# The MLP up projection with the activations stationary instead of the weights, its result turned by 32x32 block transposes and transfers inside SBUF

## The chip, the cores and the metric

The kernel runs on one core of one Trainium2 chip. The metric is the device time of one execution in microseconds (us), as the median of several runs. The rows below come from one profiled execution.

## The reference, cut to what matters

A two-layer decoder trunk on 256 tokens of width 2048, in float32. Each layer is a normalised attention mixer with a residual, and after it a normalised squared-ReLU MLP with a residual:

```python
D_MODEL = 2048; SEQ = 256; DEPTH = 2; D_FF = 4 * D_MODEL
def sq_relu_mlp(h, w_up, w_down):
    return jnp.square(jax.nn.relu(h @ w_up)) @ w_down
...
for layer in range(DEPTH):
    hn = rms_norm(h, ln_mix_g[layer])
    h = h + (even_mixer or odd_mixer)(hn, ...)
    hn = rms_norm(h, ln_mlp_g[layer])
    h = h + sq_relu_mlp(hn, w_mlp_up[layer], w_mlp_down[layer])
```

The change touches the MLP of both layers: up is 256 x 2048 by 2048 x 8192, down is 256 x 8192 by 8192 x 2048.

## The kernel before, in words

**Products.** Each float32 operand is split into a high part in fp32r and the rest, and three products stand for one: high x high, high x low, low x high. The normalised activations lie transposed in `xT` (128 channels of a k-tile in the partitions, the 256 tokens of both parts beside each other); `big` holds the MLP's hidden activations in the same form, `hid(b)` being the half of it that belongs to block `b`.

**Weights.** Everything that TensorE multiplies is a list of units. A weight chunk of 1 MB (four k-tiles of 512 columns) comes by one DMA on SyncE's queue into one of three `raw` buffers (`load`, L233). Each unit is half a chunk (two k-tiles): ScalarE writes its high part `wh` (L243), VectorE the rest `wl` (L244), into one of four buffers each. `run()` writes the program out by hand: before unit `u` it emits the split of unit `u + 3`, and the load of the chunk that replaces a wholly split one; then it emits the unit's matmuls. A unit yields four times, and at each yield (a slot) `bg.slot` emits up to two steps of side tasks that are due. The order on each engine is the order of emission, and so is the order of SyncE's queue.

**The MLP.** The 8192 hidden channels of a layer are 8 blocks of 1024, each of two halves `g` of 512. The order is up(0), up(1), down(0), up(2), down(1) and so on, down(7). A half of an up block goes through `b_units` (L347 to L390): the weights are stationary, and for each of 16 k-tiles and each of four groups of 128 channels the high weights meet both parts of x (512 columns, L370) and the low weights meet the high part (256 columns, L367). The result has the channels in the partitions, as down needs it. Four evacuations each add the two parts, take the squared ReLU and split it into `hid(b)` (L801 to L808). Banks 0 to 3 serve g = 0, banks 4 to 7 serve g = 1.

Down (L813) and the attention's projections go through `a_units` (L279): x is stationary, 128 tokens of it at a time, and 512 columns of weights move: six matmuls for one k-tile, one for each of three products and two token halves `hf`. The unit in the middle of a run emits them by L319, the first and the last unit by L306 to L308. The result has the tokens in the partitions. Down's four column groups `n` use banks 2n and 2n + 1.

Of the kernel before, what the change touches and what calls it, by code (L numbers as in the profile page):

```python
# [12 lines left out]
AF = mybir.ActivationFunctionType  # L13
ALU = mybir.AluOpType
AX = mybir.AxisListType

S = 256
# [3 lines left out]
KT = D // 128  # L21
# [126 lines left out]
def trunk_kernel(ctx: ExitStack, tc: tile.TileContext, x, w_up, w_down, even_w_in, even_w_out,  # L148
                 odd_w_in, odd_w_out, k_w1, k_w2, v_w1, v_w2, vec, rows, con, rot_in, ident_in, out):
    nc = tc.nc  # L150
# [4 lines left out]
    def sb(name, shape, dt=F32):  # L155
        return pool.tile(shape, dt, name=name)

    bank = [psum.tile([128, 512], F32, name=f"bank{i}") for i in range(8)]
# [7 lines left out]
    NRAW, NHL = 3, 4  # L166
    raw = [sb(f"raw{i}", [128, 2048]) for i in range(NRAW)]
    wh = [sb(f"wh{i}", [128, 1024], F32R) for i in range(NHL)]
    wl = [sb(f"wl{i}", [128, 1024], F32R) for i in range(NHL)]
    T = [sb(f"t{i}", [128, 1024]) for i in range(10)]  # L170
# [31 lines left out]
    bg = Background()  # L202


    units = []
# [6 lines left out]
    def weight_chunk(w, k0, nk, segs):  # L212

        width = sum(n for _, n in segs)
        pieces, at = [], 0
        for c0, n in segs:
            src = w[k0 * 128:(k0 + nk) * 128, c0:c0 + n].rearrange("(k p) c -> p k c", p=128)
            pieces.append((nk, width, at, n, src))
            at += n
        return chunk(pieces)  # L220
# [104 lines left out]
    def wide_units(w, segs, lhs, evac, banks, pre):  # L325


        for i0 in range(0, KT, 2):
            ci = weight_chunk(w, i0, 2, segs)
            for k in (i0, i0 + 1):  # L330
# [12 lines left out]
                            yield  # L343

                units.append((ci, (k - i0) * 1024, 1024, gen, True))

    def b_units(w, c0, rhs, evac, banks, pre=None):  # L347


        state = {}  # L350
        for i0 in range(0, KT, 4):
            ci = weight_chunk(w, i0, 4, [(c0, 512)])
            for j0 in (0, 2):
                ks = [i0 + j0, i0 + j0 + 1]

                def gen(u, ks=ks):
                    first, last = ks[0] == 0, ks[-1] == KT - 1
                    if pre:
                        pre(ks)
                    if first:  # L360
                        state["banks"] = banks()
                    h = wh[u % NHL].rearrange("p (k c) -> p k c", c=512)
                    lo = wl[u % NHL].rearrange("p (k c) -> p k c", c=512)
                    def part(j, n, lo_part):
                        o, k = state["banks"][j], ks[n]
                        if lo_part:
                            nc.tensor.matmul(o[:, :S], lo[:, n, j * 128:(j + 1) * 128], rhs(k)[:, :S], start=False,  # L367
                                             stop=last and n == 1)
                        else:
                            nc.tensor.matmul(o, h[:, n, j * 128:(j + 1) * 128], rhs(k), start=first and n == 0, stop=False)  # L370

                    if first or last:
                        for j in range(4):
                            for n in range(2):
                                part(j, n, 0)
                                part(j, n, 1)
                            if last:
                                evac(j, state["banks"][j])
                            yield
                    else:  # L380
                        steps = [(j, n) for n in range(2) for j in range(4)]
                        for i, (j, n) in enumerate(steps):
                            part(j, n, 0)
                            if i:
                                part(*steps[i - 1], 1)
                            if i == 7:
                                part(j, n, 1)
                            if i % 2:
                                yield

                units.append((ci, j0 * 512, 1024, gen, True))

    def t_units(w, c0, m, rhs, evac, pre):

# [92 lines left out]
    def rotate(name, of):  # L487
        rot[name] += 1
        return of[(rot[name] - 1) % len(of)]
# [4 lines left out]
    class Prep:  # L494
# [7 lines left out]
        def evac(self, hf, ps):  # L502
            r = self.norm.rows()
            if hf == 0 and self.src.name in owner:
                bg.need(owner[self.src.name])
            q = self.src[:, hf * 512:(hf + 1) * 512]
            sq = SQ[hf]
            nc.scalar.activation(q, ps, AF.Copy, scale=r[:, hf:hf + 1])
            nc.scalar.activation(sq, ps, AF.Square, scale=r[:, 2 + hf:3 + hf])
            nc.vector.tensor_reduce(self.ms[:, hf * 4:hf * 4 + 4], sq.rearrange("p (h d) -> p h d", h=4), AX.X, ALU.add)  # L510
            if hf == 1:
                self.task = owner[self.src.name] = bg.spawn(self.rest(), 2)
# [144 lines left out]
    heads = {}  # L657
# [103 lines left out]
                in_proj([(3 * FOX_W + blk * 512, 512)], gate_evac, n0)  # L761


    def out_proj(w, ready, norm, passes):
        def bl(k, part, hf):
            return big[:, k, part, hf * 128:(hf + 1) * 128]

        for first, last in passes:
            for n in range(NB):
                def evac(hf, ps, n=n, last=last):  # L770
                    xd = xs[:, hf, n * 512:(n + 1) * 512]
                    nc.vector.tensor_tensor(xd, ps, xd, ALU.add)
                    if last < KT:
                        return
                    norm.square(n, hf)
                    if hf == 1:
                        norm.start(n, (bank[4 + 2 * (n % 2)], bank[5 + 2 * (n % 2)]), 4)
                        if n == NB - 1:
                            norm.rtask = bg.spawn(stats(norm), 4)

                a_units(w, [(n * 512, 512)], bl, list(range(first, last)), evac, main3, ready)
# [5 lines left out]
    def mlp(layer, norm, nxt):  # L787
        up, down = w_up[layer], w_down[layer]
        NBLK = DFF // 1024

        def hid(b):
            return big[:, (b % 2) * 8:(b % 2) * 8 + 8]

        def up_units(b):
            for g in range(2):
                def evac(j, ps, g=g):
                    k = g * 4 + j
                    t, s_, q_ = T[j][:, 0:S], T[j][:, S:2 * S], T[j][:, 2 * S:3 * S]
                    if ("hid", j) in heads:
                        bg.need(heads["hid", j])  # L800
                    nc.scalar.activation(t, ps[:, S:], AF.Copy)  # L801
                    nc.vector.tensor_tensor(s_, ps[:, :S], t, ALU.add)
                    nc.vector.scalar_tensor_tensor(q_, s_, 0.0, s_, op0=ALU.max, op1=ALU.mult)  # L803

                    def rest():
                        d = hid(b)
                        nc.scalar.activation(d[:, k, 0], q_, AF.Copy)  # L807
                        nc.vector.tensor_tensor(d[:, k, 1], q_, d[:, k, 0], ALU.subtract)  # L808
                        yield 2
                    heads["hid", j] = bg.spawn(rest(), 1 + j)  # L810
                b_units(up, b * 1024 + g * 512, xr, evac, lambda g=g: bank[4:8] if g else [bank[3]] + [rotate("main", bank[0:3]) for _ in range(3)], norm.need)

        def down_units(b):  # L813
            for n in range(NB):
                bks = (bank[2 * n], bank[2 * n + 1])

                def evac(hf, ps, n=n):
                    if n == 0 and hf == 0 and b == 0:
                        bg.need(norm.rtask)
                    xd = xs[:, hf, n * 512:(n + 1) * 512]  # L820
                    nc.vector.scalar_tensor_tensor(xd, ps, norm.r2[:, hf:hf + 1], xd, op0=ALU.mult, op1=ALU.add)  # L821
                    if b < NBLK - 1:
                        return
                    if nxt is not None:
                        nxt.square(n, hf)
                        if hf == 1:
                            m = 2 * ((n + 3) % 4)
                            nxt.start(n, (bank[m], bank[m + 1]), 4)
                            if n == NB - 1:
                                nxt.rtask = bg.spawn(stats(nxt), 4)  # L830
                    else:
                        nc.sync.dma_start(out[hf * 128:(hf + 1) * 128, n * 512:(n + 1) * 512], xd)

                a_units(down, [(n * 512, 512)],
                        lambda k, part, hf: hid(b)[:, k - 8 * b, part, hf * 128:(hf + 1) * 128],
                        list(range(8 * b, 8 * b + 8)), evac, lambda bks=bks: bks,
                        lambda ks: bg.need(*[heads["hid", j] for j in range(4)]))

        for b in range(NBLK):
            up_units(b)  # L840
            if b:
                down_units(b - 1)
        down_units(NBLK - 1)
# [289 lines left out]
```

## Time and profile before

| what | value |
|---|---|
| median of 3 runs | 2297.97 us (2297.13 to 2299.61) |
| the profiled execution, its own time | 2299.28 us |
| its span in the profile | 2297.5 us |
| TensorE (matmul) busy | 2284.8 us, 99% |
| TensorE weight loads busy | 1924.0 us, 84% |
| VectorE busy | 1383.0 us, 60% |
| ScalarE busy | 1086.6 us, 47% |
| bytes moved, mean rate | 414.47 MB, 180 GB/s |
| mean granted TensorE clock | 0.999 |

Busy shares are means over the whole span. Matmuls are pipelined and overlap their weight loads, so the mean duration of one matmul is longer than the time by which it moves the next one on; the distance between starts, read from the chain that ended last, is the step.

### The profile page before, as it was taken

To read this page: it belongs to the slowest core of one execution; us is meant where nothing else is said; L and a number is where in the kernel's file an instruction comes from. 1 tells how busy PE (TensorE), PEld (TensorE's weight loads), DVE (VectorE), ACT (ScalarE), POOL (GpSimd) and SP (SyncE) were. 2 spreads that over 40 slices of the span, in tenths; PEclk is the share of its full clock that TensorE was granted. 3 is DMA by queue.
4 is the path that set the end of the run, shared out by engine and by line. 5 is a ranking of instruction groups with operands and counts; after the bars stand their busy time and mean duration, and the time that the engine had idled before them with its cause. 6 is when DMAs were issued, how large, how long until landed. Compare 5 with 4: busy or idle time off the path is not lost.

```text
span 2297.5 us, 28664 instructions
## 1 busy us (share of the span) xinstructions
PE 2284.8 (99%) x11403; PEld 1924.0 (84%) x11403; DVE 1383.0 (60%) x2075; ACT 1086.6 (47%) x1573; POOL 29.5 (1%) x28
## 2 busy tenths in 40 slices
PE   9999999999999999999999999999999999999999
PEld 7788888888888888888888888888888888888887
DVE  5565666666566566556554566756666556566564
ACT  6655554544444444444443555555444444444342
POOL 0000000000000000000000000000000000000000
PEclk9999999999999999999999999999999999999999
DMA  7455555555655555555546643335555565565654
GB/s 260 148 181 165 181 161 171 182 185 188 197 185 189 193 187 192 181 198 192 187 147 205 207 164 128 111 111 181 186 187 193 182 196 194 184 195 176 202 194 150
DMA packets 212870, 414.47 MB, mean 180 GB/s; under 512 B 10880, under 2 KB 12160, under 8 KB 212736
## 3 DMA queue, kind: packets, MB, share of 16 engines
q1 hardware_dynamic: 211728, 411.53, 55.0%
q8 instruction: 89, 1.46, 0.3%
q10 hardware_dynamic: 1008, 1.12, 0.1%
q14 instruction: 45, 0.37, 0.0%
HBM read 410.52 MB, written 2.10 MB: 180 GB/s over the span
## 4 chain that ended last, share of the span: by engine, by line
PE 97%; DVE 1%; ACT 1%; DMA 0%; issue 0%; ACTq 0%
PE bank L319 34%; PE bank L370 21%; PE bank L367 11%; PE bank L306 8%; PE bank L308 8%; PE bank L307 8%; PE bank L646 1%; PE bank L618 1%; PE bank L641 1%; PE bank L910 1%; PE bank L339 1%; PE bank L340 1%; PE bank L537 1%; DVE wl L244 1%; PE bank L455 1%; PE bank L338 1%
## 5 line engine op out<-in xcount | busy, mean ns | idle before, releaser
L244 DVE TENSOR_TENSOR wl<-raw,wh 128x1024 fp32r<-128x1024 f32 (+1 forms) x771 | 938.3, 1221 | 770.2 <-ACT wh L243 767.9
L243 ACT ACTIVATE wh<-raw 128x1024 fp32r<-128x1024 f32 (+1 forms) x771 | 812.3, 1055 | 864.9 <-PE bank L370 320.9
L370 PE MATMUL bank<-xT,wh 128*128 128x512 f32 x2048 | 707.6, 398 | 0.0
L367 PE MATMUL bank<-xT,wl 128*128 128x256 f32 x2048 | 543.5, 281 | 0.0
L370 PEld LDWEIGHTS bank<-xT,wh 128*128 128x128 f32 x2048 | 372.0, 188 | 74.9
L367 PEld LDWEIGHTS bank<-xT,wl 128*128 128x128 f32 x2048 | 386.9, 189 | 18.4
L319 PE MATMUL bank<-wh,big 128*128 128x512 f32 x1280 | 358.9, 391 | 0.0
L319 PE MATMUL bank<-wh,xT 128*128 128x512 f32 x1056 | 296.7, 394 | 0.0
L319 PEld LDWEIGHTS bank<-wh,big 128*128 128x128 f32 x1280 | 239.7, 188 | 49.1 <-DVE big L655 0.2
L306 PE MATMUL bank<-wh,big 128*128 128x512 f32 x640 | 253.1, 395 | 0.0
L308 PE MATMUL bank<-wh,big 128*128 128x512 f32 x640 | 249.7, 390 | 0.0
L307 PE MATMUL bank<-wl,big 128*128 128x512 f32 x640 | 249.6, 390 | 0.0
L319 PEld LDWEIGHTS bank<-wh,xT 128*128 128x128 f32 x1056 | 196.7, 188 | 39.2
L319 PE MATMUL bank<-wl,big 128*128 128x512 f32 x640 | 202.9, 393 | 0.0
L319 PE MATMUL bank<-wl,xT 128*128 128x512 f32 x528 | 172.7, 397 | 0.0
L308 PEld LDWEIGHTS bank<-wh,big 128*128 128x128 f32 x640 | 120.3, 188 | 25.6 <-DVE big L655 0.4
L306 PEld LDWEIGHTS bank<-wh,big 128*128 128x128 f32 x640 | 120.4, 188 | 24.3 <-ACT big L654 0.2
L319 PEld LDWEIGHTS bank<-wl,big 128*128 128x128 f32 x640 | 120.2, 188 | 24.4
L307 PEld LDWEIGHTS bank<-wl,big 128*128 128x128 f32 x640 | 120.5, 188 | 23.5
L319 PEld LDWEIGHTS bank<-wl,xT 128*128 128x128 f32 x528 | 99.2, 188 | 20.2 <-issue 0.2
L821 DVE SCALAR_TENSOR_TENSOR xs<-bank,r_m,xs 128x512 f32<-128x512 f32 x128 | 89.9, 743 | 7.8 <-PE bank L308 7.8
L807 ACT ACTIVATE big<-t 128x256 fp32r<-128x256 f32 x128 | 52.6, 415 | 81.8 <-DVE t L803 81.8
(189 smaller groups left out, 1543.3 us busy)
## 6 DMA issues: line engine op xcount, KB each, us to landing
raw<-in_w_up SPq DMA_DIRECT2D x128, 1024.0 KB, 5.3
raw<-in_w_down SPq DMA_DIRECT2D x128, 1024.0 KB, 5.1
raw<-in_even_w_in SPq DMA_DIRECT2D x48, 1024.0 KB, 5.1
raw<-in_odd_w_in SPq DMA_DIRECT2D x40, 1024.0 KB, 5.1
raw<-in_even_w_out SPq DMA_DIRECT2D x16, 1024.0 KB, 5.0
raw<-in_odd_w_out SPq DMA_DIRECT2D x16, 1024.0 KB, 5.3
raw<-in_even_w_in SPq DMA_DIRECT2D x10, 512.0 KB, 5.5
raw<-in_even_w_in SPq DMA_DIRECT2D x12, 256.0 KB, 5.1
```

The source lines that it names most:

```text
L243: nc.scalar.activation(h[:, at], r[:, at], AF.Copy)
L244: nc.vector.tensor_tensor(lo[:, at], r[:, at], h[:, at], ALU.subtract)
L306: nc.tensor.matmul(o, lhs(k, 0, hf), h[:, n], start=st, stop=False)
L307: nc.tensor.matmul(o, lhs(k, 0, hf), lo[:, n], start=False, stop=False)
L308: nc.tensor.matmul(o, lhs(k, 1, hf), h[:, n], start=False, stop=last and n == len(ks) - 1)
L319: nc.tensor.matmul(bks[hf], lhs(k, part, hf), w_[:, n], start=False, stop=False)
L338: nc.tensor.matmul(o, lhs(k, 0, hf), h[:, at], start=k == 0, stop=False)
L339: nc.tensor.matmul(o, lhs(k, 0, hf), lo[:, at], start=False, stop=False)
L367: nc.tensor.matmul(o[:, :S], lo[:, n, j * 128:(j + 1) * 128], rhs(k)[:, :S], start=False, stop=last and n == 1)
L370: nc.tensor.matmul(o, h[:, n, j * 128:(j + 1) * 128], rhs(k), start=first and n == 0, stop=False)
L807: nc.scalar.activation(d[:, k, 0], q_, AF.Copy)
L821: nc.vector.scalar_tensor_tensor(xd, ps, norm.r2[:, hf:hf + 1], xd, op0=ALU.mult, op1=ALU.add)
```

## The change

`b_units` goes. The up projection goes through `a_units` with `xl` as stationary operand: per half block and k-tile six matmuls of 512 columns, with banks 4 and 5 for g = 0, and 6 and 7 for g = 1. Its result has tokens in the partitions, and has to be turned:

- After each token half `hf`, VectorE's `blocks` transposes the bank's 4 x 4 grid of 32x32 blocks per 128 channels into half of `T[g]` (one instruction for 128x512 elements, read from PSUM in permuted order).
- When both halves are there, a side task emits sixteen transfers on SyncE's queue in four steps two slots apart (`across`): each moves 32 partitions of `T[g]`, two runs of 128 elements per partition, to another 32 partitions of `T[2 + g]`, 32 KB in all.
- Twenty-two slots after the last of the four steps (29 after the evacuation), VectorE takes the squared ReLU of the whole 128x1024 tile in place. Two slots later ScalarE writes the high part of it into `hid(b)`, and VectorE the rest.

Down of block `b` then waits for the two tasks of its own block, under keys of their own, and the evacuation of half `g` waits for the task of the block before on that half.

```diff
-    def b_units(w, c0, rhs, evac, banks, pre=None):
...
+    def blocks(dst, src):
+        nc.vector.transpose(dst.rearrange("p (q j i) -> p q j i", q=4, j=4), src.rearrange("p (j q i) -> p q j i", j=4, q=4))
+
+    def across(dst, src, a):
+        for q in range(4):
+            nc.sync.dma_start(dst[32 * q:32 * q + 32].rearrange("i (s a c) -> i s a c", a=4, c=128)[:, :, a],
+                              src[32 * a:32 * a + 32].rearrange("i (s q c) -> i s q c", q=4, c=128)[:, :, q])
...
-                def evac(j, ps, g=g):
-                    k = g * 4 + j
-                    t, s_, q_ = T[j][:, 0:S], T[j][:, S:2 * S], T[j][:, 2 * S:3 * S]
-                    if ("hid", j) in heads:
-                        bg.need(heads["hid", j])
-                    nc.scalar.activation(t, ps[:, S:], AF.Copy)
-                    nc.vector.tensor_tensor(s_, ps[:, :S], t, ALU.add)
-                    nc.vector.scalar_tensor_tensor(q_, s_, 0.0, s_, op0=ALU.max, op1=ALU.mult)
+                def evac(hf, ps, g=g):
+                    turned_, d = T[g], T[2 + g]
+                    if b:
+                        bg.need(heads["hid", b - 1, g])
+                    blocks(turned_[:, hf * 512:(hf + 1) * 512], ps)
 
                     def rest():
-                        d = hid(b)
-                        nc.scalar.activation(d[:, k, 0], q_, AF.Copy)
-                        nc.vector.tensor_tensor(d[:, k, 1], q_, d[:, k, 0], ALU.subtract)
+                        for a in range(4):
+                            across(d, turned_, a)
+                            yield 2
+                        yield 20
+                        nc.vector.scalar_tensor_tensor(d, d, 0.0, d, op0=ALU.max, op1=ALU.mult)
                         yield 2
-                    heads["hid", j] = bg.spawn(rest(), 1 + j)
-                b_units(up, b * 1024 + g * 512, xr, evac, lambda g=g: bank[4:8] if g else [bank[3]] + [rotate("main", bank[0:3]) for _ in range(3)], norm.need)
+                        q = d.rearrange("p (s j t) -> p j s t", s=8, j=4)
+                        h, lo = (hid(b)[:, 4 * g:4 * g + 4, part].rearrange("p j (s t) -> p j s t", s=8) for part in range(2))
+                        nc.scalar.activation(h, q, AF.Copy)
+                        nc.vector.tensor_tensor(lo, q, h, ALU.subtract)
+                        yield 1
+                    if hf == 1:
+                        heads["hid", b, g] = bg.spawn(rest(), 1)
+
+                a_units(up, [(b * 1024 + g * 512, 512)], xl, list(range(KT)), evac,
+                        lambda g=g: (bank[4 + 2 * g], bank[5 + 2 * g]), norm.need)
...
-                        lambda ks: bg.need(*[heads["hid", j] for j in range(4)]))
+                        lambda ks: bg.need(*[heads["hid", b, g] for g in range(2)]))
```

## Rows read from the trace of the kernel before

**Rows 1.** The page's busy times per engine over the span, and the granted TensorE clock and the DMA share in 40 slices.
```profile
PE 2284.8 (99%) x11403; PEld 1924.0 (84%) x11403; DVE 1383.0 (60%) x2075; ACT 1086.6 (47%) x1573; POOL 29.5 (1%) x28
...
PEclk9999999999999999999999999999999999999999
DMA  7455555555655555555546643335555565565654
```

**Rows 2.** The page's chain that ended last, by engine and by line.
```profile
PE 97%; DVE 1%; ACT 1%; DMA 0%; issue 0%; ACTq 0%
PE bank L319 34%; PE bank L370 21%; PE bank L367 11%; PE bank L306 8%; PE bank L308 8%; PE bank L307 8%; PE bank L646 1%; PE bank L618 1%; PE bank L641 1%; PE bank L910 1%; PE bank L339 1%; PE bank L340 1%; PE bank L537 1%; DVE wl L244 1%; PE bank L455 1%; PE bank L338 1%
```

**Rows 3.** The chain in order of time (start, us, what): the middle pieces of down(0)'s four column groups and, after up(2), of down(1)'s first.
```profile
550.54 5.44 PE bank L319 x24
561.42 5.44 PE bank L319 x24
572.30 5.44 PE bank L319 x24
583.18 5.44 PE bank L319 x24
639.14 5.44 PE bank L319 x24
```

**Rows 4.** The same view in an attention projection of layer 0, where x is stationary from `xT` and the run has 16 k-tiles.
```profile
118.54 16.32 PE bank L319 x72
```

**Rows 5.** Busy time and count of each engine, granted clock, DMA share and rate over up(2) and over down(1).
```profile
591.20:636.40 45.20, 45.20 (x258) 39.37 (x257) 25.57 (x32) 19.63 (x25) 0.00 (x0) 1.00 0.59 193
636.40:680.00 43.60, 43.60 (x194) 36.09 (x193) 27.61 (x34) 19.14 (x24) 0.00 (x0) 1.00 0.59 189
```

**Rows 6.** Groups of instructions by line and shape over the span (count, busy us, mean ns of one, idle before): TensorE.
```profile
L370 PE MATMUL bank<-xT,wh 128*128 128x512 f32 x2048 | 707.6, 398 | 0.0
L367 PE MATMUL bank<-xT,wl 128*128 128x256 f32 x2048 | 543.5, 281 | 0.0
L319 PE MATMUL bank<-wh,xT 128*128 128x512 f32 x1056 | 296.7, 394 | 0.0
```

**Rows 7.** The same view: VectorE, the splits, what the change removes, and the nearest instructions to what it adds.
```profile
L244 DVE TENSOR_TENSOR wl<-raw,wh 128x1024 fp32r<-128x1024 f32 x767 | 935.7, 1224 | 768.6 <-ACT wh L243 766.3
L803 DVE SCALAR_TENSOR_TENSOR t<-t 128x256 f32<-128x256 f32 x128 | 54.4, 425 | 4.4
L802 DVE TENSOR_TENSOR t<-bank,t 128x256 f32<-128x256 f32 x128 | 53.4, 417 | 0.0
L808 DVE TENSOR_TENSOR big<-t,big 128x256 fp32r<-128x256 f32 x128 | 51.1, 420 | 15.5 <-ACT big L807 15.5
L772 DVE TENSOR_TENSOR xs<-bank,xs 128x512 f32<-128x512 f32 x32 | 20.9, 683 | 2.7 <-PE bank L308 2.7
L565 DVE RECIPROCAL t<-t 128x128 f32<-128x128 f32 x16 | 14.9, 939 | 0.1
L563 DVE TENSOR_SCALAR t<-t 128x512 f32<-128x512 f32 x4 | 1.6, 392 | 0.0
```

**Rows 8.** The same view: ScalarE.
```profile
L243 ACT ACTIVATE wh<-raw 128x1024 fp32r<-128x1024 f32 x767 | 810.0, 1057 | 862.7 <-PE bank L370 320.9 <-PE bank L319 315.3 <-PE bank L308 188.5
L807 ACT ACTIVATE big<-t 128x256 fp32r<-128x256 f32 x128 | 52.6, 415 | 81.8 <-DVE t L803 81.8
L801 ACT ACTIVATE t<-bank 128x256 f32<-128x256 f32 x128 | 43.9, 369 | 0.0
```

**Rows 9.** Instructions in order of time in down(1) (start, us, what, idle before and its releaser): a split on ScalarE, the same split on VectorE, and the next on ScalarE.
```profile
652.78 1.06 ACT L243 ACTIVATE wh<-raw 128x1024 fp32r<-128x1024 f32 x1 [1.66 <-PE bank L319]
655.50 1.06 ACT L243 ACTIVATE wh<-raw 128x1024 fp32r<-128x1024 f32 x1 [1.66 <-PE bank L319]
...
653.87 1.23 DVE L244 TENSOR_TENSOR wl<-raw,wh 128x1024 fp32r<-128x1024 f32 x1 [1.49 <-ACT wh L243]
```

**Rows 10.** Who waited for whom from 540 to 1130 us (engine, line, what it waited for: us in total, times, longest), all of the rows of that answer.
```profile
DVE wl L244 <- ACT wh L243: 228.7, 168, 1.6
ACT wh L243 <- PE bank L370: 132.2, 81, 1.8
ACT wh L243 <- PE bank L319: 85.8, 57, 1.7
ACT wh L243 <- PE bank L308: 82.6, 50, 1.7
ACT big L807 <- DVE t L803: 33.2, 26, 1.8
DVE big L808 <- ACT big L807: 6.3, 13, 0.5
```

**Rows 11.** Transfers: a weight DMA's issue on SyncE's queue (ns min/median/max) and its time to landing in the stretch 640 to 700 us; the page's medians for the twelve weight pieces of 256 KB at the start and for the eight output transfers of 256 KB; the queue's packets, MB and share of 16 engines.
```profile
L233 SPq DMA_DIRECT2D raw<-in_w_up x8: 367/368/368, 660.6 to 699.0; - x8
DMA to landing us min/median/max: 4.9/5.2/5.5
...
raw<-in_even_w_in SPq DMA_DIRECT2D x12, 256.0 KB, 5.1
out_x<-xs SPq DMA_DIRECT2D x8, 256.0 KB, 2.6
...
q1 hardware_dynamic: 211728, 411.53, 55.0%
```

**Rows 12.** SyncE's queue at the start (start, us, what), and one of its waits in the first 40 us.
```profile
4.84 0.39 SPq L189 DMA_DIRECT2D xs<-in_x  x1
5.36 2.65 SPq L233 DMA_DIRECT2D raw<-in_even_w_in  x4
...
SPq L189 <- DMA raw<-in_even_w_in: 1.0, 1, 1.0
```

More of the change, by code (lines that the diff above doesn't have):

```diff
@@ L345, in wide_units @@
                 units.append((ci, (k - i0) * 1024, 1024, gen, True))
-    def b_units(w, c0, rhs, evac, banks, pre=None):
[L350 to L391, printed above, removed]
     def t_units(w, c0, m, rhs, evac, pre):
```

## The prediction, made before the change was run

> **What bounds the kernel now.** I read the busy times first: TensorE is busy 99% of the span, every other engine 60% or less, and its clock is granted at 90% or more in every slice [rows 1], 1.00 of the 2.4 GHz level in the MLP stretches of [rows 5]. A busy TensorE may still be a waiting one, so I read the chain that ended last: 97% of it is TensorE, and the two lines of the up projection, L370 and L367, hold 21% and 11% [rows 2]. In the MLP there is no wait to remove: in 590 us of it TensorE waits for nobody, only ScalarE and VectorE wait, for TensorE and for each other, and nobody waits for a transfer [rows 10]. So the MLP's time is the number of TensorE's steps times the length of one, and the change can gain only by shortening that sum.
>
> The step's length is the third reading. The mean durations of a matmul (398, 281, 394 ns [rows 6]) are of no use for it, because neighbours overlap. The chain in order of time gives it. Down's column groups start 10.88 us apart (561.42 less 550.54) and hold 48 matmuls each: 226.7 ns a matmul. The middle pieces say the same, 5.44 us for 24 [rows 3]. From the middle of down(0)'s last group to the middle of down(1)'s first are 55.96 us (639.14 less 583.18); one column group of 10.88 us lies in it, and the rest, **45.08 us, is up(2)**: two half blocks of 22.54 us, each 128 matmuls. The 45.20 and 43.60 us windows over up and down, both with TensorE busy throughout, agree with 45.08 and 4 x 10.88 = 43.52 [rows 5].
>
> **What the change takes away.** A half block has 16 k-tiles. Before, a k-tile is 4 x (512 + 256) = 3072 columns in eight matmuls; after, 6 x 512 = 3072 columns in six. The columns stay; two instructions with their weight loads go. Before, a k-tile costs 22.54 / 16 = 1.409 us. After, the same six matmuls on the same `xT`, in the same helper, are what the attention projections run: 72 in 16.32 us, 226.7 ns each [rows 4], so a k-tile costs 1.360 us and a half block 96 x 0.2267 = 21.76 us. Its first and last units use another order (L306 to L308), which the 10.88 us groups of down already contain at the same mean [rows 3]. The gain is 0.78 us a half block; 8 blocks, 2 halves and 2 layers make 32: **25.0 us**.
>
> The page "TensorE: Matmul & The Clock Gate" of the Trainium skill, section "Back-to-back issue gap", counts 518 cycles for 512 columns and 262 for 256 at the full clock, as an isolated gap. By it, as an estimate, a k-tile goes from 3120 to 3108 cycles, 5 ns, and the whole change gains 2.6 us. The trace differs: 226.7 ns where that count gives 216, and 352 ns for a pair of 512 and 256 where it gives 325 (1.409 / 4, worked out above).
>
> **What it adds, and what hides it.** All of it lies on engines beside TensorE, so the question is how late each may be. A split ends on VectorE 2.3 us after the unit before which it was emitted begins (ScalarE's 1.06 and VectorE's 1.23 us from 652.78 to 655.10 [rows 9]); its unit comes three units later, and a unit is 2.72 us (655.50 less 652.78). TensorE stands only if a split is later than 8.16 - 2.3 = **5.8 us**. A weight chunk is sent for when a buffer's last split ends and is first read after two more chunks, 0.4 + 4 x 2.72 = 11.3 us later; it lands after 5.2 us at the median [rows 11], so it has **6.1 us** before ScalarE waits, and 5.8 more before TensorE does.
>
> - VectorE, removed per half block: 4 x (417 + 425 + 420) ns = 5.05 us [rows 7]. Added: two block transposes of 128x512 from PSUM, a squared ReLU and a subtraction of 128x1024. The trace has no transpose on VectorE. Bounds: 0.39 us (a 128x512 with one input in SBUF) and 3.76 us (the reciprocal's 939 ns per 128 elements, four times). I take 0.68, the row that also reads 128x512 from PSUM [rows 7]. The two others are of L244's shape, 1.22 us each. Sum 3.8 us, between 3.2 and 10.0: VectorE, busy 25.6 of 45.2 us in up now, would be at most 35 of 43.5 [rows 5]. The place matters more: the second transpose is ahead of the next split. At the dear end the two finish 6.2 us after the half block (the first may start 1.36 us, half a unit, before its end), the split's part follows at 7.4, and 8.16 is when it is due. So nothing at either end.
> - The later pair stands in VectorE's queue ahead of splits too: 1.22, then ScalarE's copy of 1.06, then 1.22: 3.5 us, under 5.8. Nothing.
> - ScalarE, removed: 4 x (369 + 415) = 3.1 us; added: one copy of 128x1024, near 1.06 [rows 8]. A relief off the path.
> - SyncE's queue gets sixteen transfers per half block, 512 in all. An issue takes 0.37 us [rows 11], so 5.9 us. They stand behind a weight load that waits for a split, about 3 us into the next half block, and ahead of the next load, which is ready at 7.7 us: by issues alone it is 1.2 us late. An issue may also wait for an earlier transfer that has nothing to do with it (SyncE stood 1.0 us before an x load for a weight transfer [rows 12]). If half of the sixteen had to wait for the weight load to land, the last would leave at 3 + 5.2 + 8 x 0.37 = 11.2 us and the next load be 3.9 us late. Both are under 6.1. Nothing; with that cover gone it would be TensorE that waits.
> - The turn itself: 28 slots of 0.68 us (a quarter of a unit) after the half block, at 19 us, VectorE reads the result. The last transfer leaves by 8.9 to 11.2 us. No row shows a 32 KB transfer inside SBUF; the nearest lands in 2.6 us, 256 KB from SBUF [rows 11], and behind a weight load 5.2 or more. Landed at 11.5 to 16.4: before 19. Nothing.
> - DMA engines: 1024 packets of 512 B per half block, 64 per engine. A 2 KB packet takes 0.55 x 16 x 2297.5 / 211728 = 95 ns of an engine [rows 11]; a quarter of it to all of it makes 1.5 to 6.1 us of 21.76, on a share of 0.59 [rows 5]: 0.66 to 0.87.
> - GpSimd's queue gets and loses nothing. Banks 4 to 7 in up were last read one column group of down earlier at the nearest. The down projection's wait on its own block costs nothing: half g = 1 is due 31 slots into the down of the block before, which has 64.
>
> The Trainium skill speaks against such transfers: "DMA: Bandwidth & Descriptors", section "Measured (HBM→SBUF, 128 partitions, SWDGE, issued from GpSimd)", has transfers under 64 KB dominated by their descriptors. At the 2 us of fixed cost that "SBUF — State Buffer", section "The DMA setup-cost knee", gives, sixteen one after another would be an estimated 33 us, past the 19 us; no row here shows one.
>
> **Sum.** 2299.28 - 25.0 = 2274.3 us for the profiled execution; it lies 1.3 us above the median of 2297.97, so the median becomes **2273 us**, 1.1% less.
>
> **Rivals.**
> - *Given back in part.* At each half block the crowd of transposes, turn and splits makes TensorE stand a little, because several waits that I priced alone meet. For it: they all fall in the first units after a half block. Against: two cushions of 5.8 us or more. Half of the gain, 0.39 us each, makes 12.5 us: 2285.
> - *Columns alone count.* The step's length belongs to the place (xT, the banks), not to the instruction count, and the new half block takes 22.54 us as well: 2298, no change. Against: two different places with x stationary show 226.7 ns [rows 3, 4]. (By the count of the Trainium skill's page "TensorE: Matmul & The Clock Gate", above, this is the case, with an estimated 2295.)
> - *The turn is late (slower).* If the sixteen transfers of a half block go one after another, VectorE stands at the squared ReLU with every split behind it. Counted from 3 us, it stands when one takes over (19 - 3) / 16 = 1.0 us, and TensorE from (19 + 5.8 - 3) / 16 = 1.4 us. At 2.6 us each they end at 44.6 us, 19.8 us past that, 32 times: +634, less 25: about 2900. Against: at the start SyncE sends four weight pieces in 2.65 us [rows 12], and pieces of 256 KB land only after 5.1 us there [rows 11], so transfers do overlap.
>
> **How the numbers follow.** Chances: forecast 0.78, given back in part 0.10, columns alone 0.04, late turn 0.08. A measurement of this kernel tells about 0.2% (4.6 us) from no change. Faster by more: the first two less a little, 0.87; within: 0.05; slower: 0.08. The forecast's own range is 2273 less and more 5 (twice the 2.5 us between the fastest and slowest run before). The range goes up to take in the partial case with the same 5: **2268 to 2290**; the last two cases, 0.12, stay out.
>
> **What would show it.** Right: the up stretch of two half blocks is 43.5 us, L319 on `xT` gets 2304 matmuls more, TensorE is busy 99% of a shorter span, down stays at 10.88 us a group, no wait for a transfer in the MLP but SyncE's own. Wrong: VectorE idle in front of the squared ReLU for a transfer (late turn); ScalarE waiting for `raw` (loads late); gaps of TensorE in the first units after a half block (given back); a step over 230 ns in up with no gap (columns alone).

## The result and the profile after

The changed kernel takes 2274.47 us (median) against 2298.03 us of the kernel before, a ratio of 0.9903 with a 95% interval of 0.9882 to 0.9924. The profiled execution took 2275.63 us, its span is 2273.8 us.

The page of the changed kernel: busy times, and the chain that ended last.

```profile
PE 2261.2 (99%) x10379; PEld 1873.6 (82%) x10379; DVE 1355.2 (60%) x1819; ACT 1039.2 (46%) x1349; POOL 29.5 (1%) x28
...
PE 97%; DVE 1%; ACT 1%; DMA 0%; issue 0%; ACTq 0%
PE bank L319 57%; PE bank L308 11%; PE bank L306 11%; PE bank L307 11%; PE bank L600 1%; PE bank L572 1%; PE bank L595 1%; PE bank L339 1%; PE bank L340 1%; PE bank L338 1%; PE bank L884 1%; PE bank L491 1%; PE bank L409 1%; DVE wl L244 1%; PE bank L601 0%; DMA raw<-in_odd_w_in 0%
```

TensorE is still nearly the whole chain, and it has 1024 matmuls fewer (11403 before [rows 1]). The chain in order of time shows where the 23.7 us of the span went (down(0)'s first and last group, the two halves of up(2), down(1)'s first group):

```profile
548.47 5.44 PE bank L319 x24
...
581.11 5.44 PE bank L319 x24
591.99 16.32 PE bank L319 x72
613.75 16.32 PE bank L319 x72
635.51 5.44 PE bank L319 x24
```

From 581.11 to 635.51 are 54.40 us; less one column group of 10.88 that makes 43.52 for up(2), where [rows 3] gave 45.08. The halves are 613.75 - 591.99 = 21.76 us apart. The windows over an up and a down stretch, the answer to [rows 5], are now of equal length:

```profile
590.00:633.50 43.50, 43.50 (x193) 36.05 (x192) 23.27 (x22) 17.85 (x18) 0.00 (x0) 1.00 0.65 206
633.50:677.00 43.50, 43.50 (x193) 36.03 (x192) 27.97 (x28) 17.96 (x18) 0.00 (x0) 1.00 0.64 206
```

What the turn costs, by line and shape on VectorE and ScalarE, and SyncE's transfers (issue in ns, then time to landing in us, min/median/max):

```profile
L721 DVE STREAM_TRANSPOSE t<-bank 128x512 f32<-128x512 f32 x64 | 43.7, 700 | 0.0
L774 DVE SCALAR_TENSOR_TENSOR t<-t 128x1024 f32<-128x1024 f32 x32 | 39.0, 1218 | 0.0
L779 DVE TENSOR_TENSOR big<-t,big 128x1024 fp32r<-128x1024 f32 x32 | 38.3, 1196 | 0.0
L778 ACT ACTIVATE big<-t 128x1024 fp32r<-128x1024 f32 x32 | 33.4, 1044 | 0.0
...
L727 SPq DMA_DIRECT2D t<-t x512: 585/594/1822, 481.4 to 2195.5; - x171
DMA to landing us min/median/max: 1.8/1.9/6.9
```

SyncE's queue, then VectorE, after the half block that ends at 611.03 us (2.72 before 613.75):

```profile
611.92 2.51 SPq L727 DMA_DIRECT2D t<-t  x4
614.52 0.53 SPq L233 DMA_DIRECT2D raw<-in_w_down  x1
615.10 8.85 SPq L727 DMA_DIRECT2D t<-t  x12
...
617.60 1.23 DVE L244 TENSOR_TENSOR wl<-raw,wh 128x1024 fp32r<-128x1024 f32 x1 [1.50 <-ACT wh L243]
...
629.62 1.22 DVE L774 SCALAR_TENSOR_TENSOR t<-t 128x1024 f32<-128x1024 f32 x1
```

The last transfer is issued at 623.4 and lands 1.9 us later, 14.2 us after the half block; the squared ReLU comes at 629.62 and waits for nothing. But the second weight load, whose buffer was free at 618.83 when the split of 617.60 ended, leaves only after the twelve transfers, at 624.05: 5.2 us late. That is seen in the waits of the MLP (530 to 1110 us), the answer to [rows 10]:

```profile
DVE wl L244 <- ACT wh L243: 231.7, 194, 1.5
ACT wh L243 <- PE bank L319: 213.3, 129, 1.7
ACT wh L243 <- PE bank L308: 117.2, 78, 1.7
ACT wh L243 <- DMA raw<-in_w_down: 11.4, 5, 2.8
DVE wl L244 <- DMA t<-t: 6.0, 4, 1.5
```

ScalarE now waits for a weight load now and then, up to 2.8 us; TensorE still for nobody. The 1.5 us of the last row are VectorE's usual pause between two splits (1.50 us at 617.60 above), put down to a transfer that landed in it.

### The profile page after: what moved, and what is told of

Same layout as the page of the kernel before. It is cut to its first block, busy times and chain, and to the rows that moved or that the text cites. A ratio compares the mean times of both kernels' runs of the same rounds, so it can differ in the third digit from the quotient of the medians.

```text
span 2273.8 us, 26862 instructions
## 1 busy us (share of the span) xinstructions
PE 2261.2 (99%) x10379; PEld 1873.6 (82%) x10379; DVE 1355.2 (60%) x1819; ACT 1039.2 (46%) x1349; POOL 29.5 (1%) x28
## 3 DMA queue, kind: packets, MB, share of 16 engines
q1 hardware_dynamic: 252688, 428.34, 58.7%
## 4 chain that ended last, share of the span: by engine, by line
PE 97%; DVE 1%; ACT 1%; DMA 0%; issue 0%; ACTq 0%
PE bank L319 57%; PE bank L308 11%; PE bank L306 11%; PE bank L307 11%; PE bank L600 1%; PE bank L572 1%; PE bank L595 1%; PE bank L339 1%; PE bank L340 1%; PE bank L338 1%; PE bank L884 1%; PE bank L491 1%; PE bank L409 1%; DVE wl L244 1%; PE bank L601 0%; DMA raw<-in_odd_w_in 0%
## 5 line engine op out<-in xcount | busy, mean ns | idle before, releaser
L319 PE MATMUL bank<-wh,xT 128*128 128x512 f32 x2592 | 712.3, 391 | 0.0
L319 PEld LDWEIGHTS bank<-wh,xT 128*128 128x128 f32 x2592 | 484.9, 188 | 99.0
L319 PE MATMUL bank<-wl,xT 128*128 128x512 f32 x1296 | 409.5, 392 | 0.0
L319 PE MATMUL bank<-wh,big 128*128 128x512 f32 x1280 | 358.8, 391 | 0.0
L319 PEld LDWEIGHTS bank<-wl,xT 128*128 128x128 f32 x1296 | 243.4, 188 | 50.1 <-issue 0.2
L319 PEld LDWEIGHTS bank<-wh,big 128*128 128x128 f32 x1280 | 239.6, 188 | 49.2 <-DVE big L609 0.2
L308 PE MATMUL bank<-wh,big 128*128 128x512 f32 x640 | 249.5, 390 | 0.0
L319 PE MATMUL bank<-wl,big 128*128 128x512 f32 x640 | 202.8, 393 | 0.0
L306 PE MATMUL bank<-wh,xT 128*128 128x512 f32 x432 | 171.1, 396 | 0.0
L308 PE MATMUL bank<-wh,xT 128*128 128x512 f32 x432 | 168.4, 390 | 0.0
L307 PE MATMUL bank<-wl,xT 128*128 128x512 f32 x432 | 168.1, 389 | 0.0
L308 PEld LDWEIGHTS bank<-wh,big 128*128 128x128 f32 x640 | 120.3, 188 | 25.5 <-DVE big L609 0.4
L319 PEld LDWEIGHTS bank<-wl,big 128*128 128x128 f32 x640 | 120.3, 188 | 24.5
L308 PEld LDWEIGHTS bank<-wh,xT 128*128 128x128 f32 x432 | 81.1, 188 | 17.1
L307 PEld LDWEIGHTS bank<-wl,xT 128*128 128x128 f32 x432 | 81.3, 188 | 16.1
```

Source lines behind the costliest of these rows:

```text
L306: nc.tensor.matmul(o, lhs(k, 0, hf), h[:, n], start=st, stop=False)
L307: nc.tensor.matmul(o, lhs(k, 0, hf), lo[:, n], start=False, stop=False)
L308: nc.tensor.matmul(o, lhs(k, 1, hf), h[:, n], start=False, stop=last and n == len(ks) - 1)
L319: nc.tensor.matmul(bks[hf], lhs(k, part, hf), w_[:, n], start=False, stop=False)
```

## The experiments

e2, e3, e5, e7 and e8 are single executions. They differ from the kernels that they are compared with by 41.6 us or more; the executions of one kernel differ by up to 8.3 us here.

**Is the turn wholly hidden? e1_no_turn**

```diff
-                    blocks(turned_[:, hf * 512:(hf + 1) * 512], ps)
+                    nc.vector.tensor_copy(d[:, hf * 512:(hf + 1) * 512], ps)
-                        for a in range(4):
-                            across(d, turned_, a)
-                            yield 2
+                        yield 8
```

> The changed kernel without its turn: VectorE copies the banks into the tile as they are instead of transposing them, and the sixteen transfers are left out (the hidden activations are then in the wrong order). Theory (the gain is TensorE's step alone, and the turn is wholly hidden): the same 2273 to 2275 us as the changed kernel, up halves of 21.76 us, no wait of ScalarE for raw in the MLP. Rival (part of the gain is given back by the turn): faster than the changed kernel by the part given back, 1 us or more, at most the 1.3 us that the sum of 25.0 lacks.

Measured: 2274.48 us, ratio to before 0.9892 (0.9872 to 0.9912), beside 2274.47 with the turn. The medians alone could hide a us or two. The chain does not: layer 0's MLP, from the last group of `out_proj` to the first group of what follows, in the kernel before, the changed kernel and e1:

```profile
449.53 4.81 PE bank L319 x21
1138.14 4.81 PE bank L319 x21
...
450.21 4.81 PE bank L319 x21
1126.71 4.81 PE bank L319 x21
...
449.90 4.81 PE bank L319 x21
1126.40 4.81 PE bank L319 x21
```

That is 688.61, 676.50 and again 676.50 us: the 512 transfers, and a transposed reading of the bank instead of a plain one, cost TensorE nothing. (VectorE's own time is not tested by e1, as the 64 copies take 683 ns each and the transposes 700.) ScalarE's waits from 530 to 1110 us are again all for TensorE (221.3 us for L319, 120.4 for L308).

**What makes the old step long? e2_low_512, e3_halves, e9_grouped.** First the kernel before with its narrow matmuls made wide:

```diff
-                            nc.tensor.matmul(o[:, :S], lo[:, n, j * 128:(j + 1) * 128], rhs(k)[:, :S], start=False,
+                            nc.tensor.matmul(o, lo[:, n, j * 128:(j + 1) * 128], rhs(k), start=False,
```

> The kernel before, with the low weights meeting both parts of x as well: eight matmuls of 512 columns per k-tile, weights stationary (adds the product low x low). Theory (a matmul of 512 columns takes 226.7 ns whatever is stationary, and it is the 256-column one that costs more than its columns, 352.2 less 226.7 = 125.5 ns): a half block takes 16 x 8 x 0.2267 = 29.0 us, the whole 2298 + 32 x 6.5 = 2505 us. Rival (matmuls with the weights stationary are the dear ones, by the chain's 0.2348 us for each of 512 columns): 30.05 us a half block, 2538 us.

Measured: 2505.66 us. The chain, from the middle of a down's last group to that of the next down's first:

```profile
609.74 5.44 PE bank L319 x24
...
678.64 5.44 PE bank L319 x24
```

68.90 - 10.88 = 58.02 us for 256 matmuls: 226.6 ns each. Weights or x stationary, 512 columns take the same time. Then the changed kernel with narrow matmuls:

```diff
-                                    nc.tensor.matmul(bks[hf], lhs(k, part, hf), w_[:, n], start=False, stop=False)
+                                    for j in range(cut):
+                                        c_s = slice(j * width // cut, (j + 1) * width // cut)
+                                        nc.tensor.matmul(bks[hf][:, c_s], lhs(k, part, hf), w_[:, n, c_s], start=False, stop=False, skip_group_check=cut > 1)
...
+                        lambda g=g: (bank[4 + 2 * g], bank[5 + 2 * g]), norm.need, cut=2)
```

> The changed kernel with every matmul of the up projection cut into two of 256 columns: twelve per k-tile, x stationary, the columns unchanged. Theory (a 256-column matmul costs 125.5 ns): 24.1 us a half block, 2274 + 32 x 2.34 = 2349 us. Rival 1 (columns alone count): no change, 2274. Rival 2 (with only 256 columns to hide behind, each 188 ns weight load sets the step): 36.1 us a half block, 2733 us.

Measured: 2316.11 us, 41.6 more than the changed kernel, and none of the three numbers. Its chain over the two halves of an up block, which start 23.03 us apart:

```profile
596.86 17.28 PE bank L325 x144
619.89 17.28 PE bank L325 x144
```

17.28 / 144 = 120.0 ns for 256 columns, 106.7 less than the 226.7 for 512. So 256 columns more cost 106.7 ns, which is one column per cycle at the 2.4 GHz that the clock rows grant (1.00); 512 are then 213.3, and both matmuls cost their columns **plus 13.3 ns**. Rival 2 falls too: with 6144 narrow matmuls the weight loads, 191 ns each here, set no step of 188. Six matmuls more per k-tile at 13.3 ns make 16 x 32 x 6 x 13.3 ns = 40.9 us, and 41.6 were measured. So of the change's 25.0 us, the two matmuls that go per k-tile are 13.7; the other 11.3 are the old pair's 352.2 ns less 226.7 + 120.0, 5.5 ns for each pair. The last run asks whether these come of wide and narrow taking turns:

```diff
+                    for i, (j, n) in enumerate(steps):
+                        part(j, n, 0)
+                        if i in (3, 7):
+                            yield
+                    for i, (j, n) in enumerate(steps):
+                        part(j, n, 1)
+                        if last and n == 1:
+                            evac(j, state["banks"][j])
+                        if i in (3, 7):
+                            yield
```

> The kernel before, with each unit's eight matmuls of 512 columns first and its eight of 256 after them, instead of taking turns; same instructions and columns. From the runs so far every matmul costs its columns at 2.4 GHz plus 13.3 ns (226.7 ns for 512; 120.0 ns for 256 in the changed kernel with halves), and a pair of 512 and 256 that take turns costs 352.2, 5.5 ns more than the sum of 346.7. Theory (these 5.5 ns come of the two widths taking turns): grouped, a half block falls by 64 x 5.5 x 7/8 = 0.31 us, the whole by 9.9 us to 2288. Rival 1 (a 256-column matmul with its own weights as stationary operand costs 125.5 ns whatever its neighbours): 2298. Rival 2 (a run of 256-column matmuls on fresh weights cannot hide 188 ns weight loads, as these hide only behind the wide ones): slower than before.

Measured: 2293.46 us, ratio 0.9982 (0.9973 to 0.9992): faster by 4.5 us where the theory has 9.9, between it and its first rival.

```profile
604.72 1.84 PE bank L370 x8
607.52 1.84 PE bank L370 x8
```

A unit takes 2.80 us (from one start to the next), where 8 x 226.7 + 8 x 120.0 ns make 2.77 and the old order took 2.82 (an eighth of 22.54). The eight narrow ones take 0.96 us of it, 120 ns each with the weights stationary too; the eight wide ones take 1.84 where 8 x 226.7 ns are 1.81, so what is left lies in them. Taking turns does cost something, but one group of each width leaves about half of it, so a change of width is dearer when it is rare, or something else is in it. What the other half is stays open.

**How much cover has the turn? e4_delay8, e5_delay0.** The slots before the squared ReLU are cut.

```diff
-                        yield 20
+                        yield 8
```

> The changed kernel with 8 slots instead of 20 before the squared ReLU. VectorE then reaches it 10.5 us after the half block's end, and the transfers land some 14.2 us after it in the changed kernel. Theory (TensorE is covered for 5.8 us): VectorE stands about 3.7 us per half block for the transfers and the time stays at 2274 us. Rival (the cover is smaller than worked out): each half block loses up to 3.7 us, 2274 to 2390.

Measured: 2276.77 us, ratio to before 0.9904 (0.9875 to 0.9932), the changed kernel's own ratio. VectorE stands before all 32 squared ReLUs, 3.5 us each, and TensorE takes no notice:

```profile
DVE t L774 <- DMA t<-t: 110.9, 32, 5.1
```

```diff
-                        yield 20
```

> The changed kernel with no slots but the last transfers' two before the squared ReLU: VectorE reaches it 5.0 us after the half block's end and stands till the transfers land at 14.2, about 9 us. The split queued behind it is then ready at 16.6 us, and TensorE wants it at 13.6. Theory: TensorE stands 3 to 5 us per half block, 2370 to 2434 us. Rival (a late turn is hidden anyway, since the hidden activations are only needed a block later): 2274.

Measured: 2397.93 us, 3.9 us more for each half block, as the theory has it. VectorE stands 9.1 us each, TensorE 2.6:

```profile
DVE t L773 <- DMA t<-t: 292.1, 32, 10.7
PE bank L319 <- DVE wl L244: 82.2, 32, 4.1
```

Most of the other 1.3 us is the clock. The run's mean granted clock is 0.985, the changed kernel's 0.998: 0.013 of 2396 us is 1.0 us for each half block. It does not fall at every gap. Behind the gap that ends at 645.8 us TensorE is busy, with a mean granted clock of 0.76, a mixture of its two levels (2.4 and 1.2 GHz), and takes 6.84 us for 24 matmuls instead of 5.44. From 744.6 to 1017.7 us TensorE is idle for 12.1 us in gaps, and the clock stays at 1.00. What sets the two apart was not tried:

```profile
645.80:652.70 6.90, 6.84 (x24) 5.53 (x25) 5.84 (x6) 3.90 (x5) 0.00 (x0) 0.76 0.81 242
744.60:1017.70 273.10, 261.03 (x1145) 214.19 (x1143) 148.73 (x141) 102.79 (x100) 0.00 (x0) 1.00 0.61 194
```

So the cover lies between the 3.5 us that were free and the 9.1 that cost 2.6, as 5.8 us would have it (9.1 less 5.8 is 3.3).

**Whose turn does down wait for? e8_latest**

```diff
-                        lambda ks: bg.need(*[heads["hid", b, g] for g in range(2)]))
+                        lambda ks: bg.need(*[heads["hid", min(b + 1, NBLK - 1), g] for g in range(2)]))
```

> The changed kernel with the old rule for the down projection: down of block b is emitted only after the tasks of block b + 1, the latest, are emitted. The transfers, the squared ReLU and the split of its second half then stand right at the end of up, ahead of the next splits on VectorE. Theory: VectorE stands for the transfers till about 14.8 us after the half block, the next split is ready at 19.5, TensorE wants it at 10.9: 8.6 us of gap at each of 14 downs, 2394 us (2380 to 2430). Rival (the rule makes no difference, as a task's emission is only moved): 2274.

Measured: 2438.43 us, 164 more, 11.7 for each of 14 downs, and above the 2380 to 2430 expected. TensorE stands 7.8 us for ScalarE and 0.7 for VectorE, close to the 8.6 expected:

```profile
PE bank L306 <- ACT wh L243: 108.6, 14, 8.8
PE bank L307 <- DVE wl L244: 9.2, 14, 0.7
```

The remaining 3.3 us are mostly the clock. Around one such gap (TensorE's first matmul behind it, and then windows) the granted clock goes from 1.00 to 0.50, the level of 1.2 GHz, while TensorE is idle for 7.45 us; it is 0.50 in 5 us in which TensorE is busy throughout, and then comes back:

```profile
662.88 0.80 PE L306 MATMUL bank<-wh,big 128*128 128x512 f32 x1 [7.45 <-ACT wh L243]
```

```profile
641.00:656.50 15.50, 14.44 (x64) 11.63 (x62) 6.30 (x7) 3.08 (x3) 0.00 (x0) 1.00 0.67 200
656.50:664.30 7.80, 0.80 (x1) 0.29 (x1) 3.61 (x4) 3.47 (x4) 0.00 (x0) 0.69 0.08 18
664.30:669.40 5.10, 5.07 (x12) 4.01 (x13) 4.70 (x5) 1.37 (x2) 0.00 (x0) 0.50 0.58 178
669.40:675.00 5.60, 5.60 (x25) 4.58 (x25) 2.45 (x2) 2.12 (x2) 0.00 (x0) 0.98 0.63 213
```

Twelve matmuls take 5.1 us in it instead of 2.7, which is 2.4 of the 3.3 us. The trace agrees with what the Trainium skill has in "TensorE: Matmul & The Clock Gate", section "Part 1: The HAM clock gate (the "warmup" mystery)", that an idle TensorE is put back to half its clock and has to work at that before it gets the full one; the gap's price goes by these rows.

**Who eats the loads' cover? e6_pool_queue, e7_twice**

```diff
-            nc.sync.dma_start(dst[32 * q:32 * q + 32].rearrange("i (s a c) -> i s a c", a=4, c=128)[:, :, a],
+            nc.gpsimd.dma_start(dst[32 * q:32 * q + 32].rearrange("i (s a c) -> i s a c", a=4, c=128)[:, :, a],
```

> The changed kernel with the sixteen transfers of each turn issued from GpSimd's queue instead of SyncE's. Theory (the loads that ScalarE waits for in the changed kernel are late because SyncE's queue is issuing transfers, and VectorE's and TensorE's cushions hide that): time unchanged at 2273 to 2275 us, ScalarE's wait for raw<-in_w_down (30.0 us over the run) gone, the loads' median landing back near 5.2 us. Rival (the DMA engines themselves are crowded): ScalarE's waits for raw stay at 20 us or more.

Measured: 2275.83 us, ratio 0.9895 (0.9879 to 0.9911), 0.8 us above the theory's stretch and within the changed kernel's own executions (2273.23 to 2281.25). In the MLP ScalarE no longer waits for any weight load, though the same 431.2 MB cross the same DMA engines (busy for 59.2% of the span, 58.7% in the changed kernel) and each transfer now takes 4.1 us to land instead of 1.9:

```profile
ACT wh L243 <- PE bank L319: 221.6, 134, 1.7
ACT wh L243 <- PE bank L308: 119.7, 80, 1.7
...
raw<-in_w_down SPq DMA_DIRECT2D x128, 1024.0 KB, 5.3
t<-t POOLq DMA_DIRECT2D x512, 32.0 KB, 4.1
```

```diff
                             across(d, turned_, a)
+                            across(T[4 + g], turned_, a)
...
-                        yield 20
+                        yield 34
```

> The changed kernel with every transfer of the turn issued twice (the second copy into a tile that nobody reads) and 34 slots instead of 20 before the squared ReLU. At 0.594 us an issue SyncE is busy with 32 of them for 19 us, and the second weight load after a half block, due at 7.7 us, leaves at about 20.4: 12.7 us late against a cover of 6.1 + 5.8 = 11.9. Theory (SyncE's queue is what eats the cover): TensorE stands 1 to 2 us per half block, 2300 to 2340 us, and ScalarE's waits for raw come to 6 us or so per half block, 200 us in all. Rival (SyncE's queue has far more room than that): 2274, no more waits for raw than the 30 us of the changed kernel.

Measured: 2530.35 us, a loss of 256 us where at most 66 were foreseen. The direction is the theory's, the size is not. SyncE's queue after the half block that ends at 750.7 us:

```profile
751.54 5.35 SPq L727 DMA_DIRECT2D t<-t  x8
756.99 0.53 SPq L233 DMA_DIRECT2D raw<-in_w_down  x1
757.57 16.75 SPq L727 DMA_DIRECT2D t<-t  x24
774.41 1.63 SPq L233 DMA_DIRECT2D raw<-in_w_down  x3
```

The load leaves 23.7 us after the half block, not 20.4: with its gap one transfer takes 0.64 us, the queue stood 0.7 us for the load in flight, and one issue took 1.42 us (at 769.05 in the chain). Once it has left it lands in 5.40 us, so it is the queue and not the doubled bytes that makes it late. That is 16 us late where the cover is 11.9, and behind it come the standing and the clock (0.71 from 783 to 790 us):

```profile
ACT wh L243 <- DMA raw<-in_w_down: 448.6, 71, 15.3
PE bank L319 <- ACT wh L243: 166.2, 32, 7.6
```

5.2 us of standing per half block, and 8.0 in all (256 / 32). ScalarE's waits are 14.0 us per half block, not 6.

## Why the prediction was right, step by step

- *The bound.* Right: TensorE was and is 97% of the chain, and the time fell with its steps.
- *The gain.* A half block of 21.76 us was forecast and measured. Of the 25.0 us the span shows 23.7. Layer for layer the profiles show 12.11 us for layer 0's MLP (688.61 before, 676.50 after) and 12.10 for layer 1's (708.76, 696.66), where 12.48 were foreseen. In layer 0 the missing 0.37 lies at the first two up blocks (2.75 us gained there, 3.12 foreseen), where the norm's transposes stand between the matmuls; it is no cost of the turn, as e1's MLPs take the same 676.50 and 696.66, and its cause was not tried. Another 0.7 us are lost before the first MLP begins (450.21 us, 449.53 before). TensorE's clock in the first 20 us is 0.91 in this profiled execution (before: 1.00), but e6, with 0.91 too, begins its MLP at 449.90 as e1 does with 1.00, so the clock alone does not explain it. That e1's span is shorter still, 2272.1, comes from the mixer between the two MLPs (437.0 us, 438.5 in the changed kernel, whose clock is 0.98 from 1400 to 1500 us where e1's is 1.00), not from the turn.
- *The reason behind the gain* was only half told. "Two instructions with their weight loads go" is 13.7 us of it by e3's 13.3 ns; the rest is what a wide and a narrow matmul lose together, of which e9 got 4.5 us back. The sum did not need this, because it took both steps whole from the rows.
- *VectorE and ScalarE.* 0.70 us for a transpose (0.68 taken), 1.22, 1.20 and 1.04 for the others: right, and the 5.8 us of cover agree with e4 and e5, which bracket it.
- *SyncE's queue* was mis-sized. An issue was taken at 0.37 us, the row of a weight load; the transfers' own row is 0.594. Hence the next load is 5.2 us late, not 1.2 to 3.9 (the prediction's own sum gives 11.2 - 7.7 = 3.5 for the upper end), and the cover of 6.1 is nearly spent, in some places overspent. So one of the prediction's signs of being wrong came: ScalarE waits for `raw`, 11.4 us from 530 to 1110 us and 30.0 over the run. "Both are under 6.1. Nothing" was right for the time by the second cover, the 5.8 us behind the first, and not by the first: e6 takes these waits away, and the time stays.
- *The turn* lands 14.2 us after the half block, inside the 11.5 to 16.4 foreseen, with 4.4 us to spare. The sixteen take 13.4 us from the first issue to the last landing, 0.84 us each, and the late turn needed 1.0.
- *DMA share.* 0.65 in up, just under the 0.66 to 0.87 foreseen.
- *The rivals.* Given back in part: refuted by e1, to 0.01 us in each MLP. Columns alone: refuted by the 13.3 ns of e3; the count of 518 and 262 cycles in the Trainium skill's "TensorE: Matmul & The Clock Gate", section "Back-to-back issue gap", is 216 and 109 ns, and the steps here are 226.7 and 120.0. Late turn: real, but only with its slots taken away (e5) or with down made to wait for the wrong block (e8).

## What to carry to other kernels

Where TensorE is never idle, count its steps: read a step as the distance of starts in the chain, for each form of matmul that the kernel already runs, and a change of the stationary operand can be priced before it is made; here 25.0 us were forecast and 23.6 measured. Then price every helper by how late it may be, in the order of its queue, and count a queue's own issue time from the nearest *kind* of transfer, not from the nearest queue. When a cover runs out, expect to pay more than the gap: 2.6 us of standing cost 3.9 in e5, where the clock fell at some of the gaps, and 8.4 cost 11.7 in e8, where it was 0.50 behind the gap shown.

## What the runs showed of the hardware that was not expected

- A matmul of 256 or 512 fp32r columns with a weight load of its own costs its columns at 2.4 GHz plus 13.3 ns in runs of one width: 512 take 226.7 ns with x stationary and 226.6 with the weights, 256 take 120.0 and 120. A 512 and a 256 that take turns cost 5.5 ns more than the two.
- SyncE spends 0.37 us on issuing a 1 MB weight load to 128 partitions (0.53 right behind the transfers), and 0.594 us on 32 KB between two groups of 32 partitions; GpSimd spends 0.535 us on the latter, and there it lands after 4.1 us instead of 1.9.
